# A hybrid encoder layer on one core: the first norm from rows of x squared on ScalarE, three pieces of x issued by ScalarE, the first evacuation two units later

## The chip, the core and the metric

The kernel runs on one core of a Trainium2 chip. The metric is the device time of one execution in microseconds (us). Before the change the median of three timed runs is 1924.5 us (1920.08 to 1925.37). One more execution was recorded by the profiler. All rows below are of that one.

## What is computed

The layer holds 256 tokens of 2048 features and computes, in this order:

```python
x = x + 0.5 * swiglu(rms_norm(x, g1), w1a, w3a, w2a)     # FFN 1, inner width 5632
h = rms_norm(x, gm); q, k, v, u, y = split(h @ w_in)
A = attention(q, k, v); R = (lru_fwd(conv(u)) + lru_bwd(conv(u))) * gelu(y)
x = x + concat([A, R]) @ w_out
x = x + 0.5 * swiglu(rms_norm(x, g2), w1b, w3b, w2b)     # FFN 2
x = x + sigmoid(rms_norm(x, gp) @ w_gate) * (p @ w_ple)
out = rms_norm(x, gf)
# rms_norm(x, g) = x * rsqrt(mean(x*x, -1) + 1e-6) * g;  swiglu(h) = (silu(h @ w1) * (h @ w3)) @ w2
```

Everything is in float32. The change touches only how the opening of FFN 1 is carried out.

## The kernel before

**Layout.** x is kept transposed in `xs`: features on the 128 partitions, 16 blocks of 128 features, 256 tokens along each. A product is computed in *units*: one unit takes one block of 128 output features over the 16 blocks of input features (function `unit`, L129). Its weights, 1 MB, come in one load into a `raw` tile of the pool `wraw`, which has three buffers. Each half of it (8 blocks, 128x1024) is split into two float32r parts: ScalarE casts the high part `whi` (L81), VectorE subtracts to get the low part `wlo` (L82). The split halves lie in a pool of four pairs. Then TensorE runs, for each half, 8 matmuls with the high part (L113, 512 columns) and 8 with the low part (L115, 256 columns) into one of four `acc` banks of PSUM. One load waits for VectorE's L82 to be done with the old content of its `raw` buffer.

**The norm.** The gain g is multiplied into x while x is split (`split_gain`, L84 to L86: ScalarE L85 writes the high part of `aT`, VectorE L86 the low part). The factor 1/rms of a token is a factor of a column of the product, so it is applied only when a unit is evacuated: `total` (L142) adds the two halves of the bank into an SBUF tile, and then the tile is multiplied by `rB`, the factors broadcast to all partitions (L287, L291).

**The opening, `lead` (L236).** Three units, (w1, block 0), (w3, block 0) and (w1, block 1), run side by side over pieces of 1, 1, 2, 4, 4 and 4 input blocks (`PIECES`), so that TensorE can start with the first piece. For each piece SyncE's queue (SP) issues the weights of the first unit, the piece of x, and the weights of the other two units. All loads of the kernel are issued by SP in one order. After the pieces GpSimd (POOL) squares x in four tensor operations of 128x1024 (L265) and adds them pairwise (L268). In `inv_rms` (L201) TensorE sums the squares over the partitions with products against a column of ones (L208), VectorE and GpSimd form (mean + eps)^-0.5 (L198, L199), VectorE makes two diagonal matrices `dg` of it (L216), TensorE multiplies these with ones to broadcast them into `rows` (L217), and ScalarE copies `rows` to `rB` (L221).

**After the opening.** `ffn` (L276) goes through 44 blocks of two units each. The first three units are those of `lead`. The next two are (w3, block 1) and (w1, block 2).

**Order.** The program is written in a single order, and a planner with a simulated clock decides in which order each engine's instructions stand in its queue. Each engine then works through its queue strictly in that order.

Of the kernel before, what the change touches and what calls it, by code (L numbers as in the profile page):

```python
# [10 lines left out]
F32 = mybir.dt.float32  # L11
F32R = mybir.dt.float32r
BF16 = mybir.dt.bfloat16
AF = mybir.ActivationFunctionType
ALU = mybir.AluOpType
# [3 lines left out]
P = 128  # L19
D = 2048  # L20
S = 256
NH = S // P
FF = 5632
C = 512
NKD = D // P
# [11 lines left out]
N_PAR = 168  # L37

WARM = 8
PIECES = 1, 1, 2, 4, 4, 4  # L40
LEAD = (0, 0), (1, 0), (0, 1)
RAW, SPL, MID, TOK, ATT, TMP, ACC = 3, 4, 17, 4, 4, 6, 4


@with_exitstack
def hymba_layer(ctx, tc, xT, pT, w1a, w3a, w2a, win, wqkv, lruw, wout, w1b, w3b, w2b,
                wgate, wple, par, qkg, rope, out):
    nc = tc.nc

    const = ctx.enter_context(tc.tile_pool(name="const", bufs=1))  # L50
    wraw = ctx.enter_context(tc.tile_pool(name="wraw", bufs=RAW))
# [4 lines left out]
    sml = ctx.enter_context(tc.tile_pool(name="sml", bufs=4))  # L56
    acc = ctx.enter_context(tc.tile_pool(name="acc", bufs=ACC, space=PSUM))
    trp = ctx.enter_context(tc.tile_pool(name="trp", bufs=8 - ACC, space=PSUM))
# [4 lines left out]
    def flat(ap):  # L63
        return ap.rearrange("p a b -> p (a b)")

    def mtile(name):
        return mid.tile([P, 4, S], F32, tag="mid", name=name)

    def tmp(name):
        return tok.tile([P, S], F32, tag="tmp", name=name, bufs=TMP)  # L70

    def par_at(at):
        return par_sb[:, at:at + 1]
# [6 lines left out]
    def split(src, hi, lo, eng=None):  # L80
        nc.scalar.copy(hi, src)  # L81
        (eng or nc.vector).tensor_tensor(lo, src, f32(hi), op=ALU.subtract)  # L82

    def split_gain(src, gain, hi, lo):  # L84
        nc.scalar.activation(hi, src, AF.Copy, scale=gain)  # L85
        nc.vector.scalar_tensor_tensor(lo, src, gain, f32(hi), op0=ALU.mult, op1=ALU.subtract)  # L86
# [6 lines left out]
    loads, jobs = [], []  # L93

    def tick():
        for job in list(jobs):
            if next(job, job) is job:
                jobs.remove(job)

    def load(dst, src):  # L100
        loads.append(nc.sync.dma_start(dst, src))  # L101

    def spl_pair():
        return (wspl.tile([P, 8, P], F32R, tag="whi", name="whi"),
                wspl.tile([P, 8, P], F32R, tag="wlo", name="wlo"))


    def unit_mms(ps, ws, acts, first, last):


        n = len(ws)
        for i in range(n):
            nc.tensor.matmul(ps, lhsT=ws[i][0], rhs=acts[i], start=first and i == 0, stop=False)  # L113
        for i in range(n):
            nc.tensor.matmul(ps[:, 1, :], lhsT=ws[i][1], rhs=acts[i][:, 0, :], start=False,  # L115
                             stop=last and i == n - 1)

    def weights(src, nk):
        raw = wraw.tile([P, 16, P], F32, tag="raw", name="raw")
        load(flat(raw[:, :nk, :]), src)  # L120
        got = []
        for j in range(0, nk, 8):
            n = min(8, nk - j)
            hi, lo = spl_pair()
            split(raw[:, j:j + n, :], hi[:, :n, :], lo[:, :n, :])
            got += [(hi[:, i, :], lo[:, i, :]) for i in range(n)]
        return got

    def unit(aT, srcs, nk):  # L129

        ps = acc.tile([P, 2, S], F32, tag="acc", name="acc")
        at, n = 0, nk * len(srcs)
        for src in srcs:
            ws = weights(src, nk)
            for j in range(0, nk, 8):
                part = ws[j:j + 8]
                unit_mms(ps, part, aT[at:at + len(part)], at == 0, at + len(part) == n)
                at += len(part)
        tick()
        return ps  # L140
# [27 lines left out]
    def act_tiles():  # L168
        ts = [act.tile([P, 4, 2, S], F32R, tag="aT", name="aT") for _ in range(4)]
        return [ts[k // 4][:, k % 4, :, :] for k in range(NKD)]  # L170
# [3 lines left out]
        return [ts[k // 2][:, k % 2, :, :] for k in range(n)]  # L174


    warm = sml.tile([P, 1], F32, tag="warm", name="warm", bufs=1)
    nc.gpsimd.memset(warm, 0.0)
    nc.scalar.activation(warm, warm, AF.Silu)
# [3 lines left out]
    for _ in range(WARM):  # L183
        nc.tensor.matmul(idle, lhsT=zero[:, :P], rhs=zero, start=True, stop=True)

    par_sb = const.tile([P, N_PAR], F32, name="par_sb")
    xs = const.tile([P, NKD, S], F32, name="xs")
    ident = const.tile([P, P], F32, name="ident")
    make_identity(nc, ident)
    ones = const.tile([P, P], F32, name="ones")  # L190
# [4 lines left out]
    def rsqrt(dst, ssum, n, width):  # L195

        v = sml.tile([P, 8], F32, tag="rs_v", name="rs_v")[:, :width]
        nc.vector.tensor_scalar(v, ssum, 1.0 / n, EPS, op0=ALU.mult, op1=ALU.add)  # L198
        nc.gpsimd.tensor_tensor(dst, v, mhalf[:, :width], op=ALU.pow)  # L199

    def inv_rms(*ssq, halves=range(NH), keep=True):  # L201


        ps = trp.tile([P, 2, S], F32, tag="tr", name="sums")
        n = len(halves)
        for i, h in enumerate(halves):
            for j, s in enumerate(ssq):
                nc.tensor.matmul(ps[:, 0, i:i + 1], lhsT=s[:, h * P:(h + 1) * P], rhs=ones[:, 0:1],  # L208
                                 start=j == 0, stop=j == len(ssq) - 1)
        r = sml.tile([P, NH], F32, tag="inv", name="inv", bufs=2)[:, :n]  # L210
        rsqrt(r, ps[:, 0, :n], D, n)
        dg = tmp("dg")
        pb = trp.tile([P, 2, S], F32, tag="tr", name="rows")
        for i in range(n):
            cols = slice(i * P, (i + 1) * P)
            nc.vector.tensor_scalar(dg[:, cols], ident, r[:, i:i + 1], None, op0=ALU.mult)  # L216
            nc.tensor.matmul(pb[:, 0, cols], lhsT=ones, rhs=dg[:, cols], start=True, stop=True)  # L217
        if not keep:
            return r, pb[:, 0, :n * P]
        rB = sml.tile([P, S], F32, tag="rB", name="rB", bufs=2)  # L220
        nc.scalar.copy(rB, pb[:, 0, :])  # L221
        return r, rB
# [12 lines left out]

    def lead():  # L236

        aT = act_tiles()
        ps = [acc.tile([P, 2, S], F32, tag="acc", name="acc") for _ in LEAD]
        at = 0  # L240
        for n in PIECES:
            if at % 8 == 0:
                sp = [spl_pair() for _ in LEAD]
                raw = [mid.tile([P, 8, P], F32, tag="mid", name="lead") for _ in LEAD]
            js = slice(at % 8, at % 8 + n)
            for m, (i, b) in enumerate(LEAD):
                load(flat(raw[m][:, js, :]), (w1a, w3a)[i][b, 0, :, at * P:(at + n) * P])
                if m == 0:
                    if at == 0:
                        load(par_sb, par)  # L250
                    load(flat(xs[:, at:at + n, :]), xT[:, at * S:(at + n) * S])
            for m in range(len(LEAD)):
                split(raw[m][:, js, :], sp[m][0][:, js, :], sp[m][1][:, js, :])
                if m == 0:
                    for k in range(at, at + n):
                        split_gain(xs[:, k, :], par_at(O_G1 + k), aT[k][:, 0, :], aT[k][:, 1, :])
            for m in range(len(LEAD)):
                unit_mms(ps[m], [(sp[m][0][:, k % 8, :], sp[m][1][:, k % 8, :]) for k in range(at, at + n)],
                         aT[at:at + n], at == 0, at + n == NKD)
            at += n  # L260
        sq = []
        for g in range(4):
            t = flat(mtile("sq"))
            part = flat(xs[:, 4 * g:4 * g + 4, :])
            nc.gpsimd.tensor_tensor(t, part, part, op=ALU.mult)  # L265
            sq.append(t)
            if g % 2:
                nc.gpsimd.tensor_tensor(t, sq[g - 1], t, op=ALU.add)  # L268
        ssq = [t[:, k * S:(k + 1) * S] for t in sq[1::2] for k in range(4)]
        return aT, inv_rms(*ssq), dict(zip(LEAD, ps))  # L270

    def next_block(aT, n, gain_at, ssq):
        split_gain(xs[:, n, :], par_at(gain_at + n), aT[n][:, 0, :], aT[n][:, 1, :])
# [144 lines left out]
    for g in range(2):  # L418
        u = mtile("uc")
        for k in range(4):  # L420
            ps = unit(am, [win[4 * g + k, 0]], NKD)
            t = tmp("us")
# [32 lines left out]
    for h in range(NH):  # L455
        nc.scalar.activation(v_sb[:, h, :], pkv[h][:, 2 * HD:], AF.Copy, scale=rm[:, h:h + 1])
        t = tok.tile([P, C], F32, tag="tok", name="ks")
# [74 lines left out]
    for qc in range(2):  # L532
        pq = proj(am, [wqkv[qc, k] for k in range(4)])
        qro, qsc = [], []
        for h in range(NH):
            t = tok.tile([P, C], F32, tag="tok", name="qs")
# [18 lines left out]
    for g in range(2):  # L555
        y = mtile("y")
        for k in range(4):
            ps = unit(am, [win[8 + 4 * g + k, 0]], NKD)
            t = tmp("ys")
# [6 lines left out]
    for n in range(NKD):  # L566
        ps = unit(mixT, [wout[n, 0]], NKD)
# [13 lines left out]
    for g in range(4):  # L581
        t = mid.tile([P, 8, P], F32, tag="mid", name="wp")
# [27 lines left out]
    for n in range(NKD - 2):  # L610
        pe = embed(n)
        g = tmp("gate")
# [18 lines left out]
    for i in range(2):  # L631
        ps = trp.tile([P, S], F32, tag="tr", name="small")
        for k in range(NKD):
            nc.tensor.matmul(ps, lhsT=held[i][k][1], rhs=ap[k][:, 0, :], start=k == 0, stop=k == NKD - 1)
        t = tmp("small")
        nc.scalar.copy(t, ps)
        small.append(t)
    for h in range(NH):
        cols = slice(h * P, (h + 1) * P)
        for i in range(2):  # L640
            ps = acc.tile([P, 2, S], F32, tag="acc", name="acc")[:, :, :P]
            for k in range(NKD):
                nc.tensor.matmul(ps, lhsT=held[i][k][0], rhs=ap[k][:, :, cols], start=k == 0, stop=k == NKD - 1)  # L643
            n = NKD - 2 + i
            g = small[i][:, cols]
# [102 lines left out]
```

## Time and profile before

| | us |
|---|---|
| median of three timed runs | 1924.5 |
| lowest, highest | 1920.08, 1925.37 |
| the profiled execution | 1923.91 |
| its span, first to last instruction | 1921.8 |
| PE busy | 1879.3 (98%) |
| DVE busy | 1214.0 (63%) |
| ACT busy | 964.6 (50%) |
| POOL busy | 304.6 (16%) |

PE is TensorE's matmul side, DVE is VectorE, ACT is ScalarE, POOL is GpSimd, SP is SyncE. L82 is line 82 of the kernel. In a row of the trace, "[2.86 <-DVE aT L86]" says that the engine was idle 2.86 us before the instruction and that VectorE's line 86 ended the idle time. Times in rows are us from the start of the span. A row with x3 merges three neighbouring instructions. A busy PE may be at half of its full clock: the granted clock is 1.00 at 2.4 GHz and 0.50 at 1.2 GHz.

### The profile page before, as it was taken

What the parts mean: (1) busy time and instruction counts of PE and PEld (TensorE: products, weight loads), DVE (VectorE), ACT (ScalarE), POOL (GpSimd) and SP (SyncE); (2) the same over time, 40 slices, a digit from 0 to 9 for tenths busy, and PEclk for the clock granted to TensorE, in tenths of its full rate; (3) what the DMA queues carried; (4) which work ended last, traced back from release to release, by engine and by line L of the source; (5) the groups of instructions that cost most, each with busy time, mean ns of one, the idle gap of its engine ahead of it and who ended that gap; (6) DMA issues with size and microseconds to landing.
All of it is one profiled execution on the core that took longest, in us unless ns stands there. A gap on an engine that the chain in (4) does not pass through costs nothing.

```text
span 1921.8 us, 27287 instructions
## 1 busy us (share of the span) xinstructions
PE 1879.3 (98%) x10664; PEld 1645.7 (86%) x10664; DVE 1214.0 (63%) x1723; ACT 964.6 (50%) x1490; POOL 304.6 (16%) x231
## 2 busy tenths in 40 slices
PE   7999999999999999988999999999999999999997
PEld 6888888888888888876878888888888888888886
DVE  6756555556566556878767666655556566665686
ACT  4544444444444455686654544444444444545553
POOL 3111100001111010474201111110001111101143
PEclk8999999999999999999999999999999999999998
DMA  6555545565555456534435555554565555565642
GB/s 221 188 196 181 192 165 183 195 210 191 193 182 188 166 185 218 185 135 152 155 132 195 180 193 191 183 190 166 184 217 188 195 183 190 191 209 187 208 174 68
DMA packets 61264, 350.75 MB, mean 183 GB/s; under 512 B 6480, under 2 KB 12112, under 8 KB 31056
## 3 DMA queue, kind: packets, MB, share of 16 engines
q1 hardware_dynamic: 61136, 349.03, 53.4%
q8 instruction: 83, 1.36, 0.3%
q14 instruction: 45, 0.37, 0.1%
HBM read 346.90 MB, written 2.10 MB: 182 GB/s over the span
## 4 chain that ended last, share of the span: by engine, by line
PE 92%; DVE 3%; ACT 2%; DMA 1%; issue 1%; POOL 1%; SPq 0%; POOLq 0%; DVEq 0%; ACTq 0%
PE acc L113 59%; PE acc L115 30%; DVE wlo L82 1%; DVE gate L411 1%; ACT whi L81 0%; PE po L509 0%; DMA raw<-in_w3a 0%; PE acc L643 0%; PE pe L113 0%; SPq L101 0%; DMA lead<-in_w1a 0%; PE tr L482 0%; DMA raw<-in_wqkv 0%; DVE uc L357 0%; PE sums L208 0%
## 5 line engine op out<-in xcount | busy, mean ns | idle before, releaser
L82 DVE TENSOR_TENSOR wlo<-raw,whi 128x1024 fp32r<-128x1024 f32 x722 | 807.4, 1126 | 602.7 <-ACT whi L81 581.7
L81 ACT CAST whi<-raw 128x1024 fp32r<-128x1024 f32 x722 | 689.5, 955 | 833.1 <-PE acc L113 572.3
L113 PE MATMUL acc<-aT,whi 128*128 128x512 f32 x3296 | 835.4, 394 | 9.7 <-DVE aT L86 9.6
L113 PEld LDWEIGHTS acc<-aT,whi 128*128 128x128 f32 x3296 | 594.7, 190 | 117.8 <-DVE aT L86 12.6
L115 PEld LDWEIGHTS acc<-aT,wlo 128*128 128x128 f32 x3296 | 452.7, 191 | 32.6
L115 PE MATMUL acc<-aT,wlo 128*128 128x256 f32 x3296 | 464.4, 283 | 0.0
L113 PE MATMUL acc<-hT,whi 128*128 128x512 f32 x1408 | 364.8, 392 | 0.0
L291 POOL TENSOR_TENSOR s<-s,rB 128x256 f32<-128x256 f32 x88 | 122.8, 1396 | 1076.1 <-ACT s L288 1076.1
L113 PEld LDWEIGHTS acc<-hT,whi 128*128 128x128 f32 x1408 | 247.7, 189 | 37.2
L115 PEld LDWEIGHTS acc<-hT,wlo 128*128 128x128 f32 x1408 | 202.7, 190 | 21.3
L115 PE MATMUL acc<-hT,wlo 128*128 128x256 f32 x1408 | 209.0, 282 | 0.0
L231 POOL TENSOR_TENSOR ssq<-ssq,sqr 128x256 f32<-128x256 f32 x58 | 54.8, 944 | 339.7 <-ACT sqr L230 339.7
L113 PE MATMUL acc<-mixT,whi 128*128 128x512 f32 x256 | 64.6, 393 | 1.4 <-DVE mixT L82 1.4
L86 DVE SCALAR_TENSOR_TENSOR aT<-xs,par_sb,aT 128x256 fp32r<-128x256 f32 x64 | 48.2, 765 | 21.1 <-ACT aT L85 21.1
L113 PEld LDWEIGHTS acc<-mixT,whi 128*128 128x128 f32 x256 | 45.9, 189 | 10.2 <-DVE mixT L82 2.1
L302 DVE SCALAR_TENSOR_TENSOR xs<-acc,xs 128x256 f32<-128x256 f32 x128 | 53.6, 419 | 0.0
L85 ACT ACTIVATE aT<-xs,par_sb 128x256 fp32r<-128x256 f32 x64 | 31.6, 508 | 43.0 <-DVE xs L302 39.1
L90 PE MATMUL acc<-wlo,aT 128*128 128x512 f32 x96 | 39.9, 415 | 12.7 <-DVE wlo L82 12.7
L293 DVE TENSOR_TENSOR u<-u,s 128x256 f32<-128x256 f32 x88 | 37.4, 425 | 9.2 <-DVE u L144 0.5
L288 ACT ACTIVATE s<-z 128x256 f32<-128x256 f32 x88 | 36.7, 417 | 5.2 <-DVE z L287 5.2
L82 DVE TENSOR_TENSOR hT<-u,hT 128x256 fp32r<-128x256 f32 x88 | 38.0, 432 | 1.9 <-ACT hT L81 1.9
L287 DVE TENSOR_TENSOR z<-z,rB 128x256 f32<-128x256 f32 x88 | 37.4, 425 | 2.8
(169 smaller groups left out, 1019.2 us busy)
## 6 DMA issues: line engine op xcount, KB each, us to landing
raw<-in_w2a SPq DMA_DIRECT2D x64, 704.0 KB, 4.0
raw<-in_w1b SPq DMA_DIRECT2D x44, 1024.0 KB, 4.9
raw<-in_w3b SPq DMA_DIRECT2D x44, 1024.0 KB, 4.8
raw<-in_w2b SPq DMA_DIRECT2D x64, 704.0 KB, 4.0
raw<-in_w3a SPq DMA_DIRECT2D x43, 1024.0 KB, 4.8
raw<-in_w1a SPq DMA_DIRECT2D x42, 1024.0 KB, 4.9
raw<-in_win SPq DMA_DIRECT2D x16, 1024.0 KB, 4.9
raw<-in_wout SPq DMA_DIRECT2D x16, 1024.0 KB, 4.8
```

Of the source, the lines that this page charges most:

```text
L81: nc.scalar.copy(hi, src)
L82: (eng or nc.vector).tensor_tensor(lo, src, f32(hi), op=ALU.subtract)
L86: nc.vector.scalar_tensor_tensor(lo, src, gain, f32(hi), op0=ALU.mult, op1=ALU.subtract)
L90: nc.tensor.matmul(ps, lhsT=ah, rhs=wl, start=False, stop=False)
L113: nc.tensor.matmul(ps, lhsT=ws[i][0], rhs=acts[i], start=first and i == 0, stop=False)
L115: nc.tensor.matmul(ps[:, 1, :], lhsT=ws[i][1], rhs=acts[i][:, 0, :], start=False, stop=last and i == n - 1)
L231: (eng or nc.gpsimd).tensor_tensor(ssq[:, cols], ssq[:, cols], t, op=ALU.add)
L287: nc.vector.tensor_tensor(z, z, rB, op=ALU.mult)
L288: silu = nc.scalar.activation(s, z, AF.Silu)
L291: nc.gpsimd.tensor_tensor(s, s, rB, op=ALU.mult)
L293: nc.vector.tensor_tensor(u, u, s, op=ALU.mult)
L302: nc.vector.scalar_tensor_tensor(xs[:, n, :], ps[:, j, :], 0.5, xs[:, n, :], op0=ALU.mult, op1=ALU.add)
```

## The change

- A second copy of x, `xrow`, is given as an input, with tokens on the partitions: two tiles of 128 tokens by 2048 features, 1 MB each. They are loaded by SP into `raw` buffers, and ScalarE squares each one and adds up each token's row in the same instruction (`accum_out`). GpSimd's six operations of the opening and TensorE's sums of the opening are gone. The rest of `inv_rms` is a function of its own, `spread`, which the opening calls directly.
- The first three pieces of x (of 1, 1 and 2 blocks) and the parameters `par` are issued by ScalarE, at the very start of its queue, instead of by SP among the weights.
- After the three units of `lead` two more, (w3, block 1) and (w1, block 2), are written before the norm. The second one uses a bank of the other PSUM pool (`trp`), so that five banks are filled before the first must be evacuated.

```diff
 LEAD = (0, 0), (1, 0), (0, 1)
+MORE = (1, 1), (0, 2)
+EARLY = 3
...
-    def load(dst, src):
-        loads.append(nc.sync.dma_start(dst, src))
+    def load(dst, src, eng=None):
+        loads.append((eng or nc.sync).dma_start(dst, src))
...
-    def unit(aT, srcs, nk):
-
-        ps = acc.tile([P, 2, S], F32, tag="acc", name="acc")
+    def unit(aT, srcs, nk, other=None):
+
+        if other is not None:
+            ps = other.tile([P, 2, S], F32, tag="tr", name="acc")
+        else:
+            ps = acc.tile([P, 2, S], F32, tag="acc", name="acc")
...
+    par_sb = const.tile([P, N_PAR], F32, name="par_sb")
+    xs = const.tile([P, NKD, S], F32, name="xs")
+    at = 0
+    for n in PIECES[:EARLY]:
+        load(flat(xs[:, at:at + n, :]), xT[:, at * S:(at + n) * S], nc.scalar)
+        if at == 0:
+            load(par_sb, par, nc.scalar)
+        at += n
     warm = sml.tile([P, 1], F32, tag="warm", name="warm", bufs=1)
...
+        return spread(ps[:, 0, :n], n, keep)
+
+    def spread(sums, n=NH, keep=True):
+
         r = sml.tile([P, NH], F32, tag="inv", name="inv", bufs=2)[:, :n]
-        rsqrt(r, ps[:, 0, :n], D, n)
+        rsqrt(r, sums, D, n)
...
-                if m == 0:
-                    if at == 0:
-                        load(par_sb, par)
+                if m == 0 and p >= EARLY:
                     load(flat(xs[:, at:at + n, :]), xT[:, at * S:(at + n) * S])
...
-        sq = []
-        for g in range(4):
-            t = flat(mtile("sq"))
-            part = flat(xs[:, 4 * g:4 * g + 4, :])
-            nc.gpsimd.tensor_tensor(t, part, part, op=ALU.mult)
-            sq.append(t)
-            if g % 2:
-                nc.gpsimd.tensor_tensor(t, sq[g - 1], t, op=ALU.add)
-        ssq = [t[:, k * S:(k + 1) * S] for t in sq[1::2] for k in range(4)]
-        return aT, inv_rms(*ssq), dict(zip(LEAD, ps))
+        ps = dict(zip(LEAD, ps))
+        for i, b in MORE:
+            ps[i, b] = unit(aT, [(w1a, w3a)[i][b, 0]], NKD, trp if (i, b) != MORE[0] else None)
+        ss = sml.tile([P, NH], F32, tag="ss", name="ss", bufs=1)
+        for h in range(NH):
+            raw = flat(wraw.tile([P, 16, P], F32, tag="raw", name="raw"))
+            load(raw, xrow[h])
+            nc.scalar.activation(raw, raw, AF.Square, accum_out=ss[:, h:h + 1])
+        return aT, spread(ss), ps
```

## Rows read from the trace of the kernel before

**Rows 1.** The page's chain of work that ended last, by engine.
```profile
PE 92%; DVE 3%; ACT 2%; DMA 1%; issue 1%; POOL 1%; SPq 0%; POOLq 0%; DVEq 0%; ACTq 0%
```

**Rows 2.** Windows: length, busy PE PEld DVE ACT POOL, granted clock, DMA share, GB/s.
```profile
5.12:38.53 33.41, 24.10 (x105) 19.48 (x106) 26.44 (x35) 16.74 (x34) 13.95 (x6) 0.85 0.66 237
38.53:48.80 10.27, 10.27 (x61) 9.27 (x61) 4.49 (x8) 2.97 (x4) 0.71 (x1) 0.83 0.56 204
48.80:650.00 601.20, 601.20 (x3445) 529.08 (x3444) 362.57 (x523) 284.01 (x416) 60.54 (x44) 1.00 0.55 187
800.00:900.00 100.00, 85.94 (x422) 71.07 (x421) 80.29 (x71) 73.37 (x120) 58.59 (x27) 0.97 0.42 147
```

**Rows 3.** The chain of waits in order of time: start, length, what.
```profile
38.05 0.48 PE acc L115 x4
40.36 2.57 PE sums L208 x24
44.31 3.10 PE acc L113 x8
48.35 0.45 PE rows L217 x4
51.60 1.84 PE acc L113 x8
53.44 0.95 PE acc L115 x8
```

**Rows 4.** Timeline of VectorE in the opening: start, length, instruction, idle before.
```profile
14.17 2.86 DVE L86 SCALAR_TENSOR_TENSOR aT<-xs,par_sb,aT 128x256 fp32r<-128x256 f32 x4 [1.24 <-ACT aT L85]
16.95 1.89 DVE L82 TENSOR_TENSOR wlo<-lead,whi 128x512 fp32r<-128x512 f32 x3
18.76 9.18 DVE L86 SCALAR_TENSOR_TENSOR aT<-xs,par_sb,aT 128x256 fp32r<-128x256 f32 x4
27.86 1.88 DVE L82 TENSOR_TENSOR wlo<-lead,whi 128x512 fp32r<-128x512 f32 x3
29.66 1.66 DVE L86 SCALAR_TENSOR_TENSOR aT<-xs,par_sb,aT 128x256 fp32r<-128x256 f32 x4
...
43.96 0.48 DVE L216 TENSOR_SCALAR dg<-ident,inv 128x128 f32<-128x128 f32 x2 [0.83 <-POOL inv L199]
```

**Rows 5.** Timeline of GpSimd in the opening.
```profile
17.41 3.18 POOL L265 TENSOR_TENSOR sq<-xs 128x1024 f32<-128x1024 f32 x1 [1.84 <-DMA xs<-in_xT]
25.23 2.42 POOL L268 TENSOR_TENSOR sq<-sq 128x1024 f32<-128x1024 f32 x1
```

**Rows 6.** Timeline of TensorE's matmuls, at the start of the fourth piece.
```profile
15.90 3.32 PE L113 MATMUL acc<-aT,whi 128*128 128x512 f32 x7 [2.46 <-DVE aT L86]
```

**Rows 7.** Timeline of SP's issues.
```profile
7.36 0.43 SPq L101 DMA_DIRECT2D xs<-in_xT  x1
38.33 0.33 SPq L101 DMA_DIRECT2D raw<-in_w1a  x1
40.60 0.33 SPq L101 DMA_DIRECT2D raw<-in_w3a  x1
```

**Rows 8.** Timeline of ScalarE in the opening.
```profile
0.73 1.28 ACT L179 ACT_TABLE_LOAD   x1 [0.73 <-PEq L736]
2.79 0.30 ACT L81 CAST whi<-lead 128x128 fp32r<-128x128 f32 x1 [0.56 <-DMA lead<-in_w1a]
13.63 1.71 ACT L85 ACTIVATE aT<-xs,par_sb 128x256 fp32r<-128x256 f32 x4 [1.42 <-DMA xs<-in_xT]
```

**Rows 9.** Groups by line and form on ScalarE, whole span: count, busy us, mean ns.
```profile
L81 ACT CAST whi<-raw 128x1024 fp32r<-128x1024 f32 x594 | 623.4, 1050 | 760.2 <-PE acc L113 499.4 <-issue 237.8 <-PE acc L91 16.2
```

**Rows 10.** Windows of short stretches: columns as in group 2.
```profile
16.00:18.00 2.00, 2.00 (x5) 1.49 (x6) 2.00 (x5) 1.52 (x4) 0.59 (x1) 0.54 0.98 370
18.00:20.00 2.00, 2.00 (x9) 1.67 (x9) 2.00 (x3) 1.70 (x4) 2.00 (x1) 0.60 1.05 417
40.00:45.00 5.00, 5.00 (x37) 4.77 (x36) 1.77 (x5) 1.32 (x2) 0.71 (x1) 0.85 0.94 388
```

More of the change, by code (lines that the diff above doesn't have):

```diff
@@ L41, with hymba_layer @@
 LEAD = (0, 0), (1, 0), (0, 1)
+MORE = (1, 1), (0, 2)
+EARLY = 3
 RAW, SPL, MID, TOK, ATT, TMP, ACC = 3, 4, 17, 4, 4, 6, 4
 @with_exitstack
-def hymba_layer(ctx, tc, xT, pT, w1a, w3a, w2a, win, wqkv, lruw, wout, w1b, w3b, w2b,
+def hymba_layer(ctx, tc, xT, xrow, pT, w1a, w3a, w2a, win, wqkv, lruw, wout, w1b, w3b, w2b,
                 wgate, wple, par, qkg, rope, out):
@@ L184, in hymba_layer @@
         nc.tensor.matmul(idle, lhsT=zero[:, :P], rhs=zero, start=True, stop=True)
-    par_sb = const.tile([P, N_PAR], F32, name="par_sb")
-    xs = const.tile([P, NKD, S], F32, name="xs")
     ident = const.tile([P, P], F32, name="ident")
@@ L240, in lead @@
         at = 0
-        for n in PIECES:
+        for p, n in enumerate(PIECES):
             if at % 8 == 0:
@@ L723 @@
         "xT": _features(A(x)[0]),
+        "xrow": A(x)[0].reshape(NH, P, D),
         "pT": _features(A(p)[0, 0]),
```

## The prediction

> **What bounds the kernel now.** I read the chain of waits first: it runs through TensorE for 92% of the span [rows 1], so the time is TensorE's own work plus the places where it stands or runs slowly. The windows show where those are. From 48.80 to 650 us TensorE is busy for all of 601.20 us at full clock [rows 2]: there only fewer columns could help, and the change alters none. The first product starts at 5.12 us; from there to 38.53 TensorE is busy 24.10 of 33.41 us, and at a mean clock of 0.85. The next 10.27 us are all busy, but at 0.83.
>
> The chain in order of time gives the measure. In the steady stretch half a unit takes 1.84 + 0.95 = 2.79 us, a unit 5.58 us [rows 3]. The three units of the opening end at 38.53 (the row that starts at 38.05, plus its 0.48). Steady work begins again at 48.80, behind the broadcast product of 0.45 us, with four units done. Four units are 22.3 us of work, and 48.80 - 5.12 = 43.7 us went by: 21.4 us are lost. This is all that the change can reach.
>
> Two causes can be read off. Of VectorE's L86, four of 256 columns took 9.18 us from 18.76 on, and 2.86 us from 14.17 on, against 1.66 us for the last four at 29.66 [rows 4]. In the first case GpSimd was at its squares and sums from 17.41 to 25.23 + 2.42 = 27.65 us [rows 5]; the slow stretch ends at 27.94, 0.3 us after GpSimd does. TensorE needs each of these tiles. Then TensorE, after a wait of 2.46 us, runs at clocks of 0.54 and 0.60 [rows 6, 10], and the sums stand in its queue for 2.57 us inside (w3, block 1), after which eight matmuls take 3.10 us instead of 1.84 [rows 3].
>
> **Part 1, GpSimd's squares and TensorE's sums go.** I model when the three units would end; call it T. The fourth piece of x, the first of four blocks, is seen by ScalarE at 13.63 us [rows 8], and VectorE's L86 starts 0.54 us later [rows 4]. With a free VectorE one L86 takes 1.66 / 4 = 0.42 us, so the first tile is ready 0.96 us after the piece has landed. From there TensorE has three pieces of four blocks for three units, 36 block steps; eight steps are 2.79 us, so 36 are 12.56 us. ScalarE needs 1.71 us for four L85 and under 2 us for the casts of a piece, VectorE 1.66 + 1.88 us: each less than the 4.19 us that TensorE takes for a piece, so TensorE is the slowest from there on. The wait ahead of the fourth piece stays, and with it the low clock: 2 us at 0.54 and 2 us at 0.60 lose 0.92 + 0.80 = 1.7 us [rows 10]. I keep this, since a wait of about the same length stands before it. Bounds: none of it, or twice (3.4 us).
>
> **Part 2, pieces of x and `par` on ScalarE's queue.** SP loses four issues, all of which stand ahead of the fourth piece. One is 0.43 us and follows the next by some 0.04 us, so everything behind comes up to 4 x 0.47 = 1.9 us earlier [rows 7]. But between 5.12 and 38.53 the DMA engines were at a share of 0.66, and at 0.98 from 16 to 18 us [rows 2, 10], so they may eat part of it. Bounds 0 and 1.9; I take 1.3, because the issues were what held the transfers back at first, and the load comes later.
>
> The Trainium skill (DMA: Bandwidth & Descriptors, section "Issuing engines are not separate DMA queues") says that a second issuing engine only saves the sequencer's time, since all transfers share the same 16 engines. By that rule, where the engines are full, nothing is won, which is the second rival below; the share of 0.98 speaks for it, the lower share earlier against.
>
> On ScalarE the four issues stand ahead of the table load. The nearest price is SP's, 1.9 us; with 0.73 + 1.9 + 1.28 + 0.2 for the table load and the warming instruction its first cast is at 4.1 instead of 2.79 us [rows 8]. That is 1.3 us late, and its cover is ScalarE's idle time, of which 1.42 us lie just ahead of the fourth piece. Uncovered it would cost 1.3 us once.
>
> So T = 13.63 - 1.3 + 0.96 + 12.56 + 1.7 = 27.6 us, against 38.53.
>
> **Part 3, five units before the norm.** After T, (w3, block 1) follows without the sums, in 5.58 us, and the broadcast product of 0.45 us comes somewhere later. Four units plus the broadcast are thus done at 27.6 + 6.0 = 33.6 us, against 48.80. **Gain 15.2 us.**
>
> The two Squares cost ScalarE time. The nearest row is the cast of 1024 columns at 1.05 us [rows 9]; 2048 columns are at most twice that, 2.1 us, so 4.2 for both. They are covered by ScalarE's idle time around T (it was busy 2.97 of 10.27 us [rows 2]); if they stood right ahead of a cast that TensorE wants, up to 4.2 us. I take nothing. The added 2 MB move while the loads would stand still: in the window before, from 38.53 on, the share was 0.56.
>
> The new wait is for `raw` buffers. The second tile of rows takes the buffer of (w3, block 1), and the sixth unit, (w3, block 2), that of (w1, block 2), so both are issued only when VectorE has split those. Before, the loads that waited for these same buffers were issued at 38.33 and 40.60, that is T - 0.2 and T + 2.1 [rows 7], and 388 GB/s from 40 to 45 us are 1.94 of their 2.10 MB [rows 10]: landed at about T + 6.5, the later one 4.4 us after its issue. Cast 1.05 and L82 some 1.2 us put the sixth unit at T + 8.8, when TensorE wants it at T + 5.58 + 5.58 = T + 11.2. That is 2.4 us of slack; cost nothing. The second tile of rows lands by the same 4.4 us at T + 4.2, and its Square ends at T + 6.3. From the end of the sums at 42.93 [rows 3] to that of the diagonals at 44.44 [rows 4] it took 1.5 us, so they are ready near T + 7.8, before the fifth unit ends.
>
> The first evacuation needs no `rB`, only `total`, so banks come free in time: the sixth unit is the first that needs one, at T + 11.2.
>
> **The rivals.**
> (a) Bigger gain. TensorE at full clock, and the full 1.9 us: T = 25.3, gain 17.5 us, 1906.4.
> (b) The DMA engines eat the issues saved: the fourth piece still lands at 13.63, T = 28.9, 1910.0.
> (c) The sixth unit comes late. If the second Square stands ahead of the last cast of (w1, block 2), that cast waits for the rows: T + 6.3 + 1.05 + 1.2 = T + 8.6 before the buffer is free, 4.4 us for the load, 2.3 for the split: T + 15.3, 4.1 us late, 1913.4. For it: ScalarE takes its queue in order, and the planner's clock may think the rows early. Against: the casts are ready by T.
> (d) The broadcast product stands early in TensorE's queue, where the sums stood, 1.8 us behind T. Then TensorE waits for the diagonals till T + 7.8, that is 6.0 us, and then loses a little more to a low clock: 1916.
> (e) It isn't GpSimd that makes L86 slow, but the transfers, at 417 GB/s from 18 to 20 us [rows 10]. Then only the sums and the slow clock behind them come back, 2.57 + 1.26 us, and part of the 1.9: about 1919, at the edge of what can be told. Against: three L82 took 1.89 us from 16.95 on, under 370 GB/s, and 1.88 us at 27.86, when the loads had thinned out [rows 4].
>
> The Trainium skill (SBUF — State Buffer, section "Who interferes with whom") says that GpSimd and a VectorE instruction with two SBUF inputs take turns on a shared port pair, the second to come waiting out the whole instruction, and that DMA never holds up an engine. By that rule (e) falls; this trace agrees in the 9.18 us.
>
> (f) Slower. The planner simulates the whole program, so another opening can give another order in the mixing stage, where TensorE stood 14.06 us between 800 and 900 us [rows 2]. To undo the gain the standing time there has to grow by 15.2 us, to twice as much, and by 21 for a time that is slower by more than 0.3%. Against: from 48.80 to 650 TensorE never stands, so the work comes to that stage in the same order.
>
> **How the numbers follow.** The profiled execution took 1923.91 us, 0.6 below the median, 2.1 above its span. 1924.5 - 15.2 = 1909.3; I say 1909. Times 0.3% (5.8 us) apart can be told from no change: faster is below 1918.7, slower above 1930.3. Chances: forecast 0.50, its own range 1907 to 1911.5; (a) 0.06, (b) 0.12, (c) 0.14, (d) 0.07, (e) 0.07, (f) 0.04. All of (a) to (d) are faster, and half of (e): faster 0.90; same 0.07; slower 0.03, most of (f). The range takes in (a) to (d), with 2 to 3 us at its ends for the run to run spread: 1903.5 to 1917. Outside are (e) and (f), about 0.1.
>
> **What would show it.** Right: L86 in groups of four at 1.7 us throughout the opening; the last product of the three first units at 26 to 29 us; no L208 in the first 100 us; (w3, block 2) following (w1, block 2) with no wait beyond 0.5 us; from there on half units of 2.79 us, as before. Wrong: four L86 above 3 us with GpSimd idle (e); TensorE idle ahead of L217 (d) or ahead of the sixth unit, ended by L82 (c); more idle TensorE between 800 and 1000 us than 18 us (f). The prediction falls if T is above 33 us, or if the time that stands after the steady stretch differs from before by over 5 us.

## The result, and the profile after

The changed kernel takes 1907.59 us (median of four runs, 1907.03 to 1908.99) against 1924.34 us before (also four runs: the three behind the earlier 1924.5 and one more). The ratio is 0.9919, 95% interval 0.9907 to 0.9931: 16.8 us, or 0.8%, faster. The forecast was 1909 us, with a range of 1903.5 to 1917. The profiled execution of the changed kernel took 1907.39 us, its span is 1905.6 us, against 1923.91 and 1921.8.

The lines of the code have moved: L84 is the old L82 (low part of the weights), L87 and L88 the old L85 and L86 (x), L115 and L117 the old L113 and L115 (products with the high and the low part), L232 the old L217 (broadcast), L282 the new Square.

Windows of the kernel after, columns as in [rows 2]:

```profile
5.27:26.22 20.95, 20.23 (x97) 16.98 (x98) 16.46 (x34) 15.63 (x33) 0.00 (x0) 1.00 0.96 351
26.22:37.84 11.62, 11.62 (x70) 10.28 (x69) 5.27 (x9) 7.60 (x9) 0.71 (x1) 1.00 0.89 332
37.84:640.00 602.16, 602.16 (x3451) 529.97 (x3451) 365.22 (x528) 286.92 (x421) 61.62 (x44) 1.00 0.56 190
...
800.00:900.00 100.00, 86.79 (x398) 70.82 (x397) 80.32 (x79) 73.02 (x128) 58.80 (x27) 0.93 0.43 147
```

The stretch of the first three units was 33.41 us long and is now 20.95; GpSimd is idle in it, and the mean granted clock on record is 1.00 instead of 0.85 (for its first 5 us the rows say otherwise; see the last section). TensorE stands still for 0.7 us of it instead of 9.3. Behind it come two units and the broadcast in 11.62 us, all of it at full clock. The stretch up to 640 us is full as before, and between 800 and 900 us TensorE stands 13.2 us instead of 14.1.

The chain of waits in the opening (start, length, what):

```profile
11.79 0.52 ACT aT L87
12.31 0.02 issue
12.34 0.49 DVE aT L88
12.83 0.04 issue
12.88 2.39 PE acc L115 x7
...
25.27 0.95 PE acc L117 x8
26.22 1.84 PE acc L115 x8
...
37.39 0.45 PE rows L232 x4
37.84 1.85 PE acc L115 x8
```

The three units end at 25.27 + 0.95 = 26.22 us, against 38.53 [rows 3]. No sums stand in TensorE's queue. At 37.84 five units and the broadcast are done, so four stand at 37.84 - 5.58 = 32.26 us; before, it was 48.80. I call this the mark. It moved by 16.5 us, the span by 16.2. What comes behind the mark is 1873.0 us before and 1873.3 after, so the opening holds the whole gain.

VectorE's timeline answers to [rows 4]:

```profile
12.34 1.69 DVE L88 SCALAR_TENSOR_TENSOR aT<-xs,par_sb,aT 128x256 fp32r<-128x256 f32 x4 [1.50 <-ACT aT L87]
...
16.18 1.68 DVE L88 SCALAR_TENSOR_TENSOR aT<-xs,par_sb,aT 128x256 fp32r<-128x256 f32 x4 [0.24 <-ACT aT L87]
...
19.72 1.69 DVE L88 SCALAR_TENSOR_TENSOR aT<-xs,par_sb,aT 128x256 fp32r<-128x256 f32 x4
...
34.80 0.48 DVE L231 TENSOR_SCALAR dg<-ident,inv 128x128 f32<-128x128 f32 x2 [0.90 <-POOL inv L210]
```

All groups of four take 1.7 us, also the one that took 9.18 us. This happens while the DMA engines move 411 GB/s from 15 to 20 us, so transfers at that rate did not hold these instructions up.

ScalarE's timeline, and SP's behind the opening:

```profile
2.61 1.28 ACT L192 ACT_TABLE_LOAD   x1 [2.61 <-issue]
...
4.01 0.28 ACT L83 CAST whi<-lead 128x128 fp32r<-128x128 f32 x1
...
11.79 1.71 ACT L87 ACTIVATE aT<-xs,par_sb 128x256 fp32r<-128x256 f32 x4 [1.69 <-DMA xs<-in_xT]
...
31.68 1.92 ACT L282 ACTIVATE raw<-raw 128x2048 f32<-128x2048 f32 x1 [0.76 <-DMA raw<-in_xrow]
...
35.13 2.00 ACT L83 CAST whi<-raw 128x1024 fp32r<-128x1024 f32 x2 [1.18 <-DMA raw<-in_w3a]
```

```profile
26.53 0.33 SPq L103 DMA_DIRECT2D raw<-in_xrow  x1
...
29.02 0.33 SPq L103 DMA_DIRECT2D raw<-in_w3a  x1
```

The four issues on ScalarE put its first cast at 4.01 us, and the fourth piece of x is seen at 11.79 instead of 13.63 us. A Square over 2048 columns takes 1.92 us. The weights of the sixth unit are issued at 29.02 and cast from 35.13 on.

### The profile page after: what moved, and what is told of

Same layout as the page of the kernel before. It is cut to its first block, busy times and chain, and to the rows that moved or that the text cites. A ratio compares the mean times of both kernels' runs of the same rounds, so it can differ in the third digit from the quotient of the medians.

```text
span 1905.6 us, 27228 instructions
## 1 busy us (share of the span) xinstructions
PE 1872.7 (98%) x10632; PEld 1640.3 (86%) x10632; DVE 1203.6 (63%) x1723; ACT 965.2 (51%) x1494; POOL 292.6 (15%) x225
## 4 chain that ended last, share of the span: by engine, by line
PE 92%; DVE 3%; ACT 3%; issue 1%; POOL 1%; DMA 0%; SPq 0%; POOLq 0%; DVEq 0%; ACTq 0%
PE acc L115 59%; PE acc L117 30%; DVE wlo L84 1%; DVE gate L424 1%; DVE uc L370 0%; ACT whi L83 0%; PE po L522 0%; PE acc L656 0%; PE pe L115 0%; POOL us L437 0%; DMA xs<-in_xT 0%; PE tr L495 0%; ACT gate L403 0%; ACT a L410 0%; ACT L416 0%
## 5 line engine op out<-in xcount | busy, mean ns | idle before, releaser
L84 DVE TENSOR_TENSOR wlo<-raw,whi 128x1024 fp32r<-128x1024 f32 x722 | 806.5, 1126 | 594.7 <-ACT whi L83 577.5
L115 PE MATMUL acc<-aT,whi 128*128 128x512 f32 x3296 | 832.0, 393 | 1.2 <-DVE aT L88 1.2
L115 PEld LDWEIGHTS acc<-aT,whi 128*128 128x128 f32 x3296 | 593.1, 189 | 107.8 <-DVE aT L88 2.7
L117 PEld LDWEIGHTS acc<-aT,wlo 128*128 128x128 f32 x3296 | 451.4, 191 | 32.7
L117 PE MATMUL acc<-aT,wlo 128*128 128x256 f32 x3296 | 463.0, 283 | 0.0
L115 PE MATMUL acc<-hT,whi 128*128 128x512 f32 x1408 | 364.8, 392 | 0.0
L115 PEld LDWEIGHTS acc<-hT,whi 128*128 128x128 f32 x1408 | 247.6, 189 | 37.2
L117 PEld LDWEIGHTS acc<-hT,wlo 128*128 128x128 f32 x1408 | 202.7, 190 | 21.3
L117 PE MATMUL acc<-hT,wlo 128*128 128x256 f32 x1408 | 209.0, 282 | 0.0
L115 PE MATMUL acc<-mixT,whi 128*128 128x512 f32 x256 | 64.6, 393 | 1.4 <-DVE mixT L84 1.4
L115 PEld LDWEIGHTS acc<-mixT,whi 128*128 128x128 f32 x256 | 45.9, 189 | 10.2 <-DVE mixT L84 2.1
L87 ACT ACTIVATE aT<-xs,par_sb 128x256 fp32r<-128x256 f32 x64 | 31.5, 506 | 41.9 <-DVE xs L315 39.3
L88 DVE SCALAR_TENSOR_TENSOR aT<-xs,par_sb,aT 128x256 fp32r<-128x256 f32 x64 | 38.2, 610 | 19.4 <-ACT aT L87 19.1
L93 PE MATMUL acc<-whi,aT 128*128 128x512 f32 x96 | 39.8, 415 | 0.0
L84 DVE TENSOR_TENSOR hT<-u,hT 128x256 fp32r<-128x256 f32 x88 | 38.0, 431 | 1.9 <-ACT hT L83 1.9
```

The source lines that it names most:

```text
L93: nc.tensor.matmul(ps, lhsT=al, rhs=wh, start=False, stop=last)
```

## The experiments

In each case the mark is read from the trace: the end of the broadcast product, less 5.58 us where five units stand ahead of it; in no_more, where only three do, it is the end of the fourth unit. Each end and each mark is of one profiled execution, and the two of the same kernel (after and after_again) are 0.4 us apart. The ratio is to the kernel before, measured on the same chip.

| kernel | ratio, 95% interval | three units end, us | mark, us |
|---|---|---|---|
| before | 1 | 38.53 | 48.80 |
| before, x issued by ScalarE (x_only) | 0.9987, 0.9978 to 0.9997 | 36.25 | 44.95 |
| after, with GpSimd's squares (gps_back) | 0.9965, 0.9954 to 0.9976 | 35.04 | 41.07 |
| after, norm straight behind three units (no_more) | 0.9958, 0.9943 to 0.9972 | 27.0 | 39.0 |
| after, x issued by SP (x_on_sp) | 0.9937, 0.9920 to 0.9954 | 29.54 | 35.57 |
| after | 0.9919, 0.9907 to 0.9931 | 26.22 | 32.26 |
| after, run again (after_again) | 0.9917, 0.9904 to 0.9931 | 26.66 | 32.69 |

### GpSimd's squares put back: gps_back

```diff
+        sq = []
+        for g in range(4):
+            t = flat(mtile("sq"))
+            part = flat(xs[:, 4 * g:4 * g + 4, :])
+            nc.gpsimd.tensor_tensor(t, part, part, op=ALU.mult)
+            sq.append(t)
+            if g % 2:
+                nc.gpsimd.tensor_tensor(t, sq[g - 1], t, op=ALU.add)
         ps = dict(zip(LEAD, ps))
```

> The changed kernel with GpSimd's four squares and two sums put back where they stood, their results used by nothing. Theory (GpSimd's reads hold up VectorE's two-input instructions): one group of four of the low parts of x takes 4 to 9 us instead of 1.7, TensorE waits for it, the three units end 5 to 11 us later than 26.2, and the granted clock falls below 0.7 in some stretch: 1913 to 1919 us. Rival (the slow instructions of before came from the transfers or from their place in the order): four take 1.7 us, the end stays within 1 us of 26.2, time 1907 to 1909.

The mark moves from 32.26 to 41.07, 8.8 us later; the median is 1915.95 us. GpSimd's and VectorE's timelines:

```profile
16.70 1.90 POOL L279 TENSOR_TENSOR sq<-xs 128x1024 f32<-128x1024 f32 x1 [3.36 <-DMA xs<-in_xT]
18.55 2.54 POOL L282 TENSOR_TENSOR sq<-sq 128x1024 f32<-128x1024 f32 x1
21.05 2.07 POOL L279 TENSOR_TENSOR sq<-xs 128x1024 f32<-128x1024 f32 x1
23.20 2.43 POOL L282 TENSOR_TENSOR sq<-sq 128x1024 f32<-128x1024 f32 x1
```

```profile
11.95 2.86 DVE L88 SCALAR_TENSOR_TENSOR aT<-xs,par_sb,aT 128x256 fp32r<-128x256 f32 x4 [0.93 <-ACT aT L87]
...
17.20 8.72 DVE L88 SCALAR_TENSOR_TENSOR aT<-xs,par_sb,aT 128x256 fp32r<-128x256 f32 x4 [0.53 <-ACT aT L87]
...
27.64 1.66 DVE L88 SCALAR_TENSOR_TENSOR aT<-xs,par_sb,aT 128x256 fp32r<-128x256 f32 x4
```

Nothing uses these squares, no product waits for them, and yet the pattern of [rows 4] is back: 2.86 and 8.72 us while GpSimd runs, 1.66 us once it has ended at 25.6. Four GpSimd instructions take 8.9 us, and four VectorE instructions get through in that time, one for each: the last of them ends at 25.92, 0.3 us behind GpSimd's last at 25.63. Two of the four (L282) read only `sq` tiles, so sharing the tile `xs` with VectorE is not the cause. TensorE's clock fell to a mean of 0.81 and 0.51 in the two stretches from 20 to 30 us. This is the theory's case, and half of the gain.

### GpSimd busy without reading: gps_memset and gps_memset20

```diff
+        t = flat(mtile("sq"))
+        for g in range(20):
+            nc.gpsimd.memset(t, float(g))
         ps = dict(zip(LEAD, ps))
```

The first run had six memsets (of tiles as the squares have) at this place.

> The changed kernel with six GpSimd memsets of 128x1024 in the place of those squares and sums: GpSimd is busy and writes SBUF, but reads nothing. Theory of the Trainium skill's page SBUF (two SBUF inputs on VectorE contend with a GpSimd instruction that reads, not with one that only writes): no effect, four low parts of x in 1.7 us, 1907 to 1909 us. Rival (any GpSimd work on SBUF holds VectorE up): some group of four above 2.5 us, end of the three units over 1 us later. A memset waits for no data, so it may run earlier than the squares did.

The six ran from 1.43 to 6.85 us, ahead of the pieces of four; the groups of four took 1.68 us and the ratio was 0.9924 (0.9909 to 0.9939), but the run had missed the place. So the second one, with twenty:

> The changed kernel with twenty GpSimd memsets of one 128x1024 tile (their result used by nothing), which at 0.9 us each keep GpSimd busy writing from 1.4 to about 20 us, over the fourth and fifth piece, where the squares hurt. In the run with six they had ended before the pieces of four, so that run did not test it. Theory (only a GpSimd instruction that reads SBUF holds up VectorE's two-input instructions): groups of four low parts of x stay at 1.7 us, the three units end within 1 us of 26.2, 1907 to 1909 us. Rival (any GpSimd work does): a group of four takes 3 us or more, as with the squares, and the end is 3 to 9 us later.

GpSimd's row, and VectorE's under it:

```profile
1.43 20.19 POOL L277 MEMSET sq<- 128x1024 f32 x20
```

```profile
12.84 1.69 DVE L88 SCALAR_TENSOR_TENSOR aT<-xs,par_sb,aT 128x256 fp32r<-128x256 f32 x4 [1.49 <-ACT aT L87]
...
17.66 1.69 DVE L88 SCALAR_TENSOR_TENSOR aT<-xs,par_sb,aT 128x256 fp32r<-128x256 f32 x4 [0.53 <-ACT aT L87]
```

GpSimd was busy to 21.6 us, and both groups took 1.69 us; the ratio is 0.9916 (0.9898 to 0.9934). The three units ended at 27.33, which is 1.1 us later than in the profiled run of the changed kernel, 0.1 more than the theory allowed; after_again, the same kernel on the same chip as this run, ends at 26.66, 0.7 us sooner. The delay came with the transfers: the fourth piece of x was seen at 12.30 instead of 11.79, and the fifth piece's low parts start at 17.66 instead of 16.18 (both rows above), with VectorE idle ahead of them. Other runs with the same opening saw the fourth piece between 11.07 us (gps_memset) and 11.79. So GpSimd's being busy costs VectorE nothing; the squares, which read SBUF, do. The Trainium skill (SBUF — State Buffer, section "Who interferes with whom") states just this, for VectorE instructions with two SBUF inputs, and the two runs agree with it. The squares and the memsets differ in more than the reading, though: no run here separates it from the arithmetic.

### The x pieces: x_only, x_on_sp

The kernel before with this part alone:

```diff
+    for n in PIECES[:3]:
+        load(flat(xs[:, at:at + n, :]), xT[:, at * S:(at + n) * S], nc.scalar)
+        if at == 0:
+            load(par_sb, par, nc.scalar)
+        at += n
...
-                if m == 0:
-                    if at == 0:
-                        load(par_sb, par)
+                if m == 0 and at >= 4:
                     load(flat(xs[:, at:at + n, :]), xT[:, at * S:(at + n) * S])
```

> The kernel before with one part of the change: the first three pieces of x and the parameters issued by ScalarE. The norm stays on GpSimd and TensorE. Theory (GpSimd's squares and the sums make most of the loss): fourth piece of x near 11.8 us, but four low parts of x still take 4 to 9 us, sums still 2.6 us in TensorE's queue; gain 0.5 to 3 us, 1921 to 1924 us. Rival (the late pieces of x were the main cause): gain of 8 us or more, under 1916 us.

The mark moves by 3.9 us; the timed median is 1919.90 us against 1922.45 on the same chip, 2.6 us less (0.6 to 4.2 by the interval), and below the expected 1921 to 1924. The fourth piece is seen at 12.81 us and not near 11.8, so it came only 0.8 us sooner. VectorE still loses its turns, and TensorE still has the sums in the chain:

```profile
17.95 9.14 DVE L86 SCALAR_TENSOR_TENSOR aT<-xs,par_sb,aT 128x256 fp32r<-128x256 f32 x4
```

```profile
38.08 2.57 PE sums L214 x24
40.65 1.07 PE acc L115 x8
41.72 1.84 PE acc L113 x8
```

Much of the rest is the clock. Seven products at the fourth piece take 2.22 us instead of 3.32 [rows 6], and behind the same 2.57 us of sums the next sixteen take 1.07 + 1.84 us, where in the kernel before they took 1.38 + 3.10. Why TensorE kept its clock there in this kernel and not in the kernel before, no run shows.

The other way round, the kernel after without this part (SP issues all of x, in the order of before):

```diff
-    for n in PIECES[:EARLY]:
-        load(flat(xs[:, at:at + n, :]), xT[:, at * S:(at + n) * S], nc.scalar)
-        if at == 0:
-            load(par_sb, par, nc.scalar)
-        at += n
...
-                if m == 0 and p >= EARLY:
+                if m == 0:
+                    if at == 0:
+                        load(par_sb, par)
```

> The changed kernel with all pieces of x and the parameters issued by SyncE again; the norm and the two more units stay. Theory (issues held the transfers back): the fourth piece of x is seen 1.3 to 1.9 us later than 11.8, the wait ahead of it grows, the clock may fall: end of the three units 1.5 to 4 us later, 1909 to 1911.5 us. Rival (the DMA engines are the limit, a second issuer wins nothing): fourth piece within 0.5 us of 11.8, time 1907 to 1908.5.

The mark comes 3.3 us later, the median is 1910.15 us, 2.6 above the changed kernel. TensorE's row of the fourth piece, and the window around it:

```profile
14.62 2.85 PE L115 MATMUL acc<-aT,whi 128*128 128x512 f32 x7 [2.68 <-DVE aT L88]
```

```profile
15.00:20.00 5.00, 5.00 (x16) 3.87 (x16) 3.84 (x8) 3.52 (x9) 0.00 (x0) 0.66 1.02 372
```

The piece is seen at 13.54 instead of 11.79, which is 1.75 us. The other 1.55 us are the clock: TensorE waited 2.68 us, and then ran at 0.66 of its clock; in the kernel after it waits 0.71 us there and keeps 1.00. So in the changed kernel the part is worth what the issues save, and nearly as much again by the clock.

### Where the norm stands: no_more, more1

```diff
-MORE = (1, 1), (0, 2)
+MORE = ()
```

> The changed kernel without the two more units ahead of the norm, so that the rows of x are loaded ahead of the weights of the fourth and fifth unit, and the Squares stand ahead of their casts. Theory (the two units are what hides the rows): the three units end at 26.2 as before, then TensorE waits 3 to 6 us for the fourth unit's weights and may lose some clock: 1911 to 1915 us. Rival (the rows are hidden anyway): under 1 us of wait, 1907 to 1909 us.

The median is 1914.10 us, 6.5 above the changed kernel: the time is in the expected range, but the wait isn't only the one I expected. ScalarE's and TensorE's timelines, and a window:

```profile
26.33 1.91 ACT L282 ACTIVATE raw<-raw 128x2048 f32<-128x2048 f32 x1 [0.47 <-DMA raw<-in_xrow]
...
29.63 1.99 ACT L83 CAST whi<-raw 128x1024 fp32r<-128x1024 f32 x2 [1.04 <-DMA raw<-in_w3a]
```

```profile
29.78 1.23 PE L232 MATMUL rows<-dg,ones 128*128 128x128 f32 x4 [2.80 <-DVE dg L231]
30.73 3.78 PE L115 MATMUL acc<-aT,whi 128*128 128x512 f32 x8
34.31 1.91 PE L117 MATMUL acc<-aT,wlo 128*128 128x256 f32 x8
```

```profile
30.00:35.00 5.00, 5.00 (x16) 4.21 (x17) 4.55 (x6) 4.78 (x9) 0.50 (x1) 0.50 0.72 252
```

The broadcast stands right behind the three units, and TensorE waits 2.80 us for the diagonals, which wait for the second Square. The fourth unit's weights, which I had expected to be late, are hardly earlier: they are seen at 29.63, and their first cast ends at about 30.7, so TensorE would have stood till then even without the broadcast in its way. Then it runs at half its clock: the eight high and eight low products from 31.00 to 36.22 us take 5.2 us instead of 2.79, and the broadcast 1.23 instead of 0.45. Units written ahead are what hides the late rows: without them 6.7 of the 16.5 us are lost. With one of the two:

```diff
-MORE = (1, 1), (0, 2)
+MORE = ((1, 1),)
```

> The changed kernel with one more unit, (w3, block 1), ahead of the norm instead of two. Theory: the rows now load ahead of the weights of (w1, block 2), whose buffer and casts wait for the second Square; it comes 0 to 3 us late, 1907.5 to 1911 us. Rival (both units are needed): a wait of 3 us or more.

```profile
33.70 2.12 PE L115 MATMUL acc<-aT,whi 128*128 128x512 f32 x8 [0.48 <-ACT whi L83]
```

TensorE waits 0.48 us, for the first cast of (w1, block 2), and the clock stays. The cast stands behind the Squares in ScalarE's queue, but these were over at 31.0, and it began at 32.60. Its load was issued only at 27.62 us, when VectorE had split (w3, block 1) and so freed a buffer, and took 4.9 us: landed at 32.5. (The profile names the diagonals as what ended ScalarE's wait; they ended at 32.59, too close to the landing to tell the two apart, and in the code the cast doesn't use them.) The ratio is 0.9924 (0.9910 to 0.9939), not to be told from two units.

### Is there more in the opening: early4, early2, pieces, after_again

`EARLY = 4`, `EARLY = 2`, and the first piece of four cut in two:

```diff
-PIECES = 1, 1, 2, 4, 4, 4
+PIECES = 1, 1, 2, 2, 2, 4, 4
```

> The changed kernel with the fourth piece of x (512 KB) on ScalarE's queue too. If issuing is still what holds the fourth piece back, it is seen 0.5 to 2 us earlier than 11.8 and the three units end as much earlier, down to 1906 us; ScalarE's first cast comes 0.5 us later. If the 16 DMA engines are the limit, the weights of the first pieces come later by what the big piece takes, 1 to 1.5 us, and nothing is won or up to 1 us lost: 1907.5 to 1909 us.

> The changed kernel with only the first two pieces of x and the parameters on ScalarE's queue. By the theory that an issue costs 0.47 us of everything behind it, the fourth piece is seen 0.3 to 0.5 us later than 11.8, ScalarE's first cast 0.47 us earlier: 1907.5 to 1908.5 us. By the theory that the DMA engines are the limit: no difference.

> The changed kernel with the first piece of four blocks cut into two of two, so that TensorE need not wait for all four blocks of x and of the weights. Theory (what is left of the opening's loss is the wait for the first big piece): the product after the third piece starts 0.5 to 1.5 us earlier, the three units end up to 1 us earlier, 1906 to 1907.5 us. Rival (the 16 DMA engines set the pace, and smaller pieces move no faster): no difference or up to 1 us more.

> The changed kernel unaltered, as the neighbour on the same chip for the run with smaller pieces: 1907 to 1909 us, end of the three units at 26.2 us.

The medians are 1908.32, 1908.70, 1908.06 and 1907.89 us; the ratios of the first three 0.9924 (0.9910 to 0.9939), 0.9924 (0.9907 to 0.9941) and 0.9922 (0.9909 to 0.9934). None can be told from the changed kernel, so `EARLY = 4` and the smaller pieces came out as their second, unfavourable cases say. The median of `EARLY = 2` is 0.2 us above the expected range, which is less than its runs differ (1907.45 to 1909.37). With `EARLY = 4` the fourth piece is seen at 9.29 us, 2.5 us sooner, but the first product starts at 6.67 instead of 5.27 us, and the three units end at 26.6. With `EARLY = 2` the piece came 0.2 us later and the end at 27.4. With smaller pieces TensorE starts the fourth piece sooner and then waits 1.92 us for the next one; the end is at 27.1. From 10 to 25 us the DMA share is 0.94 to 1.05 with either value of `EARLY`: what one piece gains another gives back. This points to the transfer of the opening's 5 MB as its pace now; no run takes bytes away to show it. No version that I ran beats the changed kernel.

## Why the prediction was right

**The measure.** Four units behind the first product, 21.4 us lost, and everything behind it unchanged: the mark moved 16.5 us and the span 16.2. That the planner's new order would harm the mixing stage (rival f) didn't happen; TensorE's standing time there is within 1 us.

**Part 1.** That GpSimd's squares, and not the transfers (rival e), made four low parts take 9.18 us is shown by gps_back and by the 1.68 us at 411 GB/s; it is worth 8.8 us of the mark. The sums with the rest of the old norm are worth 3.9: that is the distance of the marks of x_only and gps_back, which differ in how the norm is computed and where it stands. The sums themselves took 0.79 + 2.57 us.

**Part 2.** The piece came 1.84 us sooner; I had put it at 1.3, between bounds of 0 and 1.9. Rival (b) is out: the issues did hold the transfers back. Where SP issues all of x the piece is seen at 13.54 and 13.63 us, in the runs with the same three pieces on ScalarE's queue at 11.07 to 12.81. ScalarE's first cast at 4.01 was forecast at 4.1, and its lateness was covered by a wait of 1.69 us ahead of the fourth piece, as argued; the first product started 0.15 us later than before.

**The clock, the term that was mis-sized.** I kept a loss of 1.7 us because a wait of about the same length would stand ahead of the fourth piece. It shrank from 2.46 to 0.71 us, and the clock stayed at 1.00: the loss is zero. I had named this as rival (a), with a chance of 0.06; its end for the three units, 25.3, is nearer than mine. So is its time, once it starts from the median like the forecast: 1924.5 - 17.5 = 1907.0 us. (I had taken rivals (a) and (b) from the profiled execution's 1923.91; (b) would be 1910.6. The chances of a faster kernel also add up to 0.925, not 0.90.) Where the wait remains the size is right: 1.55 us in x_on_sp. Against it, the 12.56 us of products and the 0.96 us ahead of them came to 14.43 us: at the first piece of four, seven products take 2.39 us instead of 1.61, as they wait for one L88 after the other. So T: 27.6 - 0.5 (transfer) - 1.7 (clock) + 0.9 = 26.3, measured 26.22.

**Part 3.** Two units and the broadcast took 11.62 us, forecast 11.6. The waits I costed at nothing cost nothing, but by less slack than I worked out: the rows of the second tile were issued at T + 0.3, the diagonals were ready at T + 9.1, not 7.8, and the sixth unit's weights landed at T + 8.9, not 6.5: they were issued 0.7 us later than I had it, and then three loads of 1 MB were under way together. Its first cast was done some 1.6 us ahead of its product. Rivals (c) and (d) were thus near: in more1 weights that waited for their buffer cost 0.48 us (a small form of (c)), in no_more the broadcast stands too early and TensorE waits 2.80 us ahead of it (d). I had added to (d) only "a little more to a low clock"; the clock cost about as much again as the wait.

How the 16.5 us of the mark divide depends on the order of the steps. From before over x_only and gps_back to after they are 3.9, 3.9 and 8.8 us; undoing single parts of the changed kernel costs 8.8 (squares), 3.3 (issues) and 6.7 us (the two units), 18.8 in all and more than the whole. These sums lean on single profiled executions. By timed medians of one chip, against gps_memset (1908.0 us; the changed kernel with six early memsets, which cannot be told from it), undoing the squares costs 8.0, the issues 2.2 and the two units 6.1 us: 16.2 in all, where the kernel before is 15.1 us slower. The order of the parts is the same, but that they bring less without one another is not shown.

## What to carry to other kernels

An instruction that is on no chain can set the pace of one that is: GpSimd reading SBUF beside VectorE subtracting two SBUF tiles let only one of VectorE's through for each of GpSimd's (2.2 us instead of 0.42), and the sign in the trace is a group whose mean is several times that of its twins elsewhere. Moving such work to another engine needs a place where its data may arrive late; look for what stands in order behind it, and write enough independent work ahead of it. A wait of TensorE can cost its length and then the clock: of the 3.3 us for the x pieces and of the 6.7 us for an early broadcast nearly half was slow running after the wait.

## What the runs showed of the hardware that was not expected

TensorE kept its full clock behind waits of 0.71 us (after), of 0.81 and 1.28 us (after_again) and of 1.92 us (pieces), and fell to 1.2 GHz behind waits of 2.68 us (x_on_sp, a mean of 0.66 over 5 us) and of 2.80 us (no_more, 0.50). But in x_only it ran at 0.50 from 9.22 to 11.10 us, behind a wait of only 1.97 us, and the kernel before kept 1.00 behind a wait of 2.86 us that ended at 11.07 us, and fell behind one of 2.46 us at 15.90 [rows 6]; the length of one wait alone doesn't decide, and what does stays open.

The granted clock on record is not always what the rows show. The first line is of the changed kernel, in a stretch recorded at 1.00; the second is of x_only, in the stretch recorded at 0.50:

```profile
8.00 1.91 PE L115 MATMUL acc<-aT,whi 128*128 128x512 f32 x4
```

```profile
9.22 1.91 PE L113 MATMUL acc<-aT,whi 128*128 128x512 f32 x4
```

Both take the same time, where five such products at full clock take 1.32 us. So the changed kernel's first products, to about 10 us, ran at half of the clock; in after_again they did not. It cost little, since the wait ahead of the fourth piece was 0.71 us in the one and 0.81 in the other.

Twenty memsets of GpSimd over 20 us left VectorE's two-input instructions at 0.42 us each, while GpSimd's squares and sums stretched them to 2.2 us.
